# The token quad beside the last softmax: the order of its third and fourth product

## The chip, the cores and the metric

The kernel runs on one core of a Trainium2 chip. The time is the device time of one execution in microseconds, lower is better. Before the change it is 1221.77 us, the median of three runs (1220.72 to 1221.81).

## The reference, cut to what matters

One layer of a hybrid encoder over a sequence of 2048 positions with 1024 channels, in float32:

```python
h = rmsnorm(x, norm_g[l])
proj = h @ w_in[l]
qk_raw, v, o, z_a, gates, u, z_b, qc, z_c = jnp.split(proj, _OFFS, axis=-1)
y_a = mlstm_branch(qk_raw, v, o, ig, fg, ...) * jax.nn.silu(z_a)
y_b = pool_branch(u, pool_w[l], pool_scale[l]) * jax.nn.silu(z_b)
y_c = mem_attn_branch(qc, mem, mem_norm_g[l], w_mem_kv[l]) * jax.nn.silu(z_c)
x = x + jnp.concatenate([y_a, y_b, y_c], axis=-1) @ w_out[l]
```

and a last RMSNorm. The memory attention is a softmax over 256 memory tokens for each of four heads. The change lies in the product `proj`, in the 512 columns of z_a, which the kernel computes while the last head's softmax runs.

## The kernel before, in words

The sequence is worked in two halves of 1024 positions (s = 0 and 1), each in two blocks of 512. The input projection is computed by a Strassen-like scheme: a product of a 2x2 block matrix (two blocks of positions, two halves of the channels) by a 2x2 block of weights is done with seven block products instead of eight. Such a group of seven is a *quad* (class `Quad`, line 224). The x operands of the seven are A11, A12, S1, S2, S3, S4, A22 and the weight operands B11, B21, T1, T2, T3, B22, N4; S and T are sums and differences of blocks. Each operand is split into a high and a low part, and each product is three matmuls for each 128 channels (`mm3`, lines 152, 155 and 156 of the page).

There are four kinds of quads. Channel quads (`qk`, `pool`, `att`) give transposed results; token quads (`tok`, i = 0 for v, 1 for o, 2 for z_a) give results by position. `run_tok` (line 390) runs a token quad: for each product n, for two PSUM banks, 24 matmuls of 128x256 a bank, 48 a product, then an eviction by ScalarE or VectorE. Seven products share four accumulators: P (A11, then A12), U (S2), V (S1, then S4), W (S3, then A22). P and V take PSUM banks of the group "mm" (four banks), U and W of "pt" (two); the other two banks are "aux" (`bank`, line 95).

The order of the products is a table, `TOK_ORDER` (line 49): A11, A12, S2, S1, S3, S4, A22. The results add up across products: the eviction of S2 makes u2 = S2 + A11 product, that of S1 makes S1 + u2, S3 adds to that, S4 and A22 add to u2. The order of the weight operands follows from the same table: `stream` (line 323) lists every form of every quad in order, `prep` (line 280) makes or loads them four forms or so ahead, as the buffers "wf" and "wr" come free when a product is done (`used`). In the first half the forms are made from raw weights (differences on GpSimd and VectorE, splits on ScalarE line 307 and VectorE line 308) and written to DRAM; in the second half they are loaded back.

In each half, `attention_stage` runs four attention quads and then the token quad i = 2 (line 921), the *tail quad*. The last attention quad hands the second block's query to `attend` (line 746), whose steps are emitted by a counter of ticks, one tick behind each bank of the tail quad: scores (two halves), transposes of the softmax output (line 776, two halves of four, into two "pt" banks), the copies of these into a high part th (ScalarE, line 781) and a low part tl (VectorE, line 782), and the product with the values (lines 152 to 156 with th and tl). With `pinned=True` the first matmul of each part of a bank keeps its place in program order.

The tile framework plans the order of instructions on every engine with a simulated timeline; program order is the priority, an instruction goes when its operands and its buffer are free in the plan. Each engine then runs its list in order.

In the second half the tail quad also has steps (`last_step`, line 999): with each product it scales and splits output weights (`prep_wo`, line 966, its work at lines 977 to 982) into the slots of x operands that are used up: the first two into those of A12, then S2, S1, S3, S4, A22. The last stage follows, an output product of 2048x1536 by 1024 columns beside the chunked mLSTM; `load_chunk` (line 1043) brings its inputs, among them qk.

Of the kernel before, what the change touches and what calls it, by code (L numbers as in the profile page):

```python
# [15 lines left out]
ALU = mybir.AluOpType  # L16
# [30 lines left out]
CH_ORDER = (("A11", "B11", "P", True), ("S2", "T2", "U", True), ("A12", "B21", "P", False),  # L47
            ("S1", "T1", "V", True), ("S3", "T3", "W", True), ("S4", "B22", "V", False), ("A22", "N4", "W", False))
TOK_ORDER = (("A11", "B11", "P", True), ("A12", "B21", "P", False), ("S2", "T2", "U", True),
             ("S1", "T1", "V", True), ("S3", "T3", "W", True), ("S4", "B22", "V", False), ("A22", "N4", "W", False))  # L50


def hybrid_block(tc, xT, xn, memT, wch, wuT, wtok, wgt, wkm, wvm, wo, pw, cols, bg, gf, out):
    nc = tc.nc
    V, A, G, T = nc.vector, nc.scalar, nc.gpsimd, nc.tensor
# [4 lines left out]
    def r32(t):  # L60
        return t.bitcast(F32)
# [7 lines left out]
    def tick():  # L69
        now[0] += 1  # L70
        ready = [f for t, f in due if t <= now[0]]
        due[:] = [(t, f) for t, f in due if t > now[0]]
        for f in ready:
            f()
# [12 lines left out]
    with ExitStack() as outer:  # L87
# [7 lines left out]
        def bank(shape, tag):  # L95
            return ps.tile(list(shape), F32, name=tag, tag=tag, bufs={"mm": 4}.get(tag, 2))
# [44 lines left out]
        def ev(name, dtype=F32, shape=(P, BW), tag=None):  # L141
            tag = tag or (name if name in ("s1", "u2") else "e")
            return ep.tile(list(shape), dtype, name=name, tag=tag, bufs=1 if tag == "e" else 2)
# [7 lines left out]
        def mm3(po, ah, al, bh, bl, first, last, pin=False):  # L151
            ins = T.matmul(po, ah, bh, start=first, stop=False, skip_group_check=True)  # L152
            if pin:
                tc.keep_in_program_order(ins)
            T.matmul(po, ah, bl, start=False, stop=False, skip_group_check=True)  # L155
            T.matmul(po, al, bh, start=False, stop=last, skip_group_check=True)  # L156
# [67 lines left out]
        class Quad:  # L224
            def __init__(self, kind, s, i):
                self.kind, self.s, self.i = kind, s, i
                self.tok = kind == "tok"
                self.order = TOK_ORDER if self.tok else CH_ORDER
                self.cost = 2 if self.tok else 1
                self.forms = {}  # L230
                self.held = {}
                self.raw = {}
                self.kept = not (self.tok and i == 0)
# [46 lines left out]
            def prep(self, f):  # L280
                if self.s and self.kept:
                    out = []
                    for kept in cache[self.kind, self.i, f]:
                        t = self.slot(f)
                        dma(r32(t).rearrange("p a b c -> p (a b c)"), kept)
                        out.append(t)
                    self.views(f, out)
                    return
                B = self.raw
                if f == "T2":  # L290
                    G.tensor_tensor(B["B11"], B["B12"], B["B11"], ALU.subtract)  # L291
                    B["T1"] = B["B11"]
                    t2 = wb.tile([P, 4, 256 if self.tok else P], F32, name="wt2", tag="wt2", bufs=1)
                    V.tensor_tensor(t2, B["B22"], B["T1"], ALU.subtract)
                    B["T2"] = t2
                if f == "T3":
                    V.tensor_tensor(B["B12"], B["B22"], B["B12"], ALU.subtract)
                    B["T3"] = B["B12"]
                if f == "N4":
                    G.tensor_tensor(B["B21"], B["B21"], B["T2"], ALU.subtract)  # L300
                    B["N4"] = B["B21"]
                src = B[f]
                out, kept = [], []
                for kk in range(self.cost):
                    t = self.slot(f)
                    part = src[:, 2 * kk:2 * kk + 2] if self.tok else src
                    A.activation(t[:, 0], part, AF.Copy)  # L307
                    V.tensor_tensor(t[:, 1], part, r32(t[:, 0]), ALU.subtract)  # L308
                    out.append(t)
                    if self.kept:  # L310
                        n = f"d_{self.kind}{self.i}{f}{kk}"
                        d = dp.tile([P, D], F32, name=n, tag=n)
                        dma(d, r32(t).rearrange("p a b c -> p (a b c)"))
                        kept.append(d)
                cache[self.kind, self.i, f] = kept
                self.views(f, out)
# [33 lines left out]
        def used(q, f):  # L350
            for tag in q.held.pop(f):
                room[tag] += 1
            pump()
# [36 lines left out]
        def run_tok(q, step=None, pinned=False):  # L390
            n_, s = q.i, q.s
            func = (AF.Copy, AF.Sigmoid, AF.Silu)[n_]
            banks = {}
            s1, u2 = [None, None], [None, None]

            def store(t, i, j, bk):
                dma_out(d_tok[2 * s + i][2 * bk:2 * bk + 2, :, n_ * GW + 256 * j:n_ * GW + 256 * j + 256].rearrange("t p w -> p t w"),
                        t.rearrange("p (t w) -> p t w", t=2))

            for n, (xfm, wfm, acc, opens) in enumerate(q.order):  # L400
                if step is not None:
                    step(n)
                if opens:
                    tag = "mm" if acc in ("P", "V") else "pt"
                    banks[acc] = [bank([P, 2, 256], tag) for _ in range(2)]
                for bk in range(2):
                    pp = banks[acc][bk]
                    for r in range(2):
                        sl = slice((2 * bk + r) * P, (2 * bk + r + 1) * P)
                        for k in range(4):  # L410
                            wh, wl = q.forms[wfm][k]
                            xt = xf[xfm][k]
                            mm3(pp[:, r], xt[:, 0, sl], xt[:, 1, sl], wh, wl, opens and k == 0 and r == 0, k == 3,
                                pin=k == 0 and (opens and r == 1 or pinned and r == 0))
                    pf = pp.rearrange("p a b -> p (a b)")
                    if n == 0:
                        s1[bk] = ev("s1")
                        A.activation(s1[bk], pf, AF.Copy)
                    elif n == 1:
                        c11 = ev("c11", tag="u2")  # L420
                        A.activation(c11, pf, func)
                        store(c11, 0, 0, bk)
                    elif n == 2:
                        u2[bk] = ev("u2")
                        V.tensor_tensor(u2[bk], pf, s1[bk], ALU.add)
                    elif n == 3:
                        V.tensor_tensor(s1[bk], pf, u2[bk], ALU.add)
                    elif n == 4:
                        t = s1[bk]
                        V.tensor_tensor(t, pf, t, ALU.add)  # L430
                        if n_:
                            A.activation(t, t, func)
                        store(t, 1, 1, bk)
                    elif n == 5:
                        t = ev("c12", tag="s1")
                        V.tensor_tensor(t, pf, u2[bk], ALU.add)
                        if n_:
                            A.activation(t, t, func)
                        store(t, 0, 1, bk)
                    else:  # L440
                        t = u2[bk]
                        V.tensor_tensor(t, pf, t, ALU.add)
                        if n_:
                            A.activation(t, t, func)
                        store(t, 1, 0, bk)
                    if bk == 1:
                        used(q, wfm)
                    tick()
# [172 lines left out]
        for n in range(12):  # L621
            later(n + 1, lambda n=n: first(n))
        it = iter(quads)
        run_tok(next(it), pinned=True)
        flush()
        close(mcm)
# [314 lines left out]
        def turn(n):  # L941
# [4 lines left out]
            else:  # L946
# [4 lines left out]
                xf.clear()  # L951
                xf.update(old)
        run_tok(next(it), turn)
        xs["A22"]()
        new["A22"] = xf["A22"]
# [309 lines left out]
```

## Time and profile before

| | |
|---|---|
| median of three runs | 1221.77 us |
| profiled execution | 1220.8 us |
| its span, first to last instruction | 1218.9 us |
| TensorE busy | 1173.5 us, 96% |
| weight loads busy (beside the matmuls) | 1016.1 us, 83% |
| VectorE busy | 743.9 us, 61% |
| ScalarE busy | 480.5 us, 39% |
| GpSimd busy | 211.5 us, 17% |
| mean granted TensorE clock | 0.983 of 2.4 GHz |

Times inside the profile are microseconds from the span's start. A matmul's duration is modelled and overlaps the next; the distance of two starts is what one costs. The tail quad's S2 starts at 406.92 in the first half and at 844.30 in the second. Behind an instruction stand in brackets the idle time of its engine ahead of it and what ended that.

### The profile page before, as it was taken

The page shows a single profiled execution, that of the slowest core. Times are in us where ns is not written, and L with a number is a line of the kernel's source. Part 1 is how long each engine was busy: PE and PEld are TensorE (multiplying, and loading weights), DVE is VectorE, ACT ScalarE, POOL GpSimd, SP SyncE. Part 2 cuts the span into 40 slices and gives each one's busy share as a digit, 9 for nine tenths or more (in the row PEclk, how much of TensorE's full clock was granted, in tenths as well). Part 3 has the DMA queues.
Part 4 walks back from the last instruction along what each step waited for, and adds up shares of the span by engine and source line. Part 5 has one row for each costly group of instructions (what it writes and reads, how often), then busy time and mean ns, then how long its engine had stood idle before and what let it go on. Part 6 is the DMA issues. An engine that isn't in the chain of part 4 may idle for free. (4 is left out here: it accounts for less than half of the span.)

```text
span 1218.9 us, 17628 instructions
## 1 busy us (share of the span) xinstructions
PE 1173.5 (96%) x6579; PEld 1016.1 (83%) x6579; DVE 743.9 (61%) x1324; ACT 480.5 (39%) x947; POOL 211.5 (17%) x154
## 2 busy tenths in 40 slices
PE   6769999999999999999999999999999999999997
PEld 5759888887888998998788888888978888888886
DVE  5966587887777559633564554554546656556444
ACT  7534544444766444331311225555433223222211
POOL 1351121112001003100000000000054423233110
PEclk9879999999999999999999999999999999999999
DMA  9618788779555796546667776446695454554411
GB/s 350 233 44 299 265 293 281 259 276 324 211 195 182 256 390 226 181 140 228 198 219 241 240 244 226 154 155 223 214 325 188 137 184 154 172 165 151 144 52 69
DMA packets 124725, 258.75 MB, mean 212 GB/s; under 512 B 9824, under 2 KB 66400, under 8 KB 124384
## 3 DMA queue, kind: packets, MB, share of 16 engines
q1 hardware_dynamic: 83232, 226.17, 53.9%
q10 hardware_dynamic: 41408, 31.46, 8.1%
q8 instruction: 52, 0.85, 0.3%
q14 instruction: 33, 0.27, 0.1%
HBM read 158.96 MB, written 98.63 MB: 211 GB/s over the span
## 5 line engine op out<-in xcount | busy, mean ns | idle before, releaser
L307 ACT ACTIVATE wf<-wr 128x512 fp32r<-128x512 f32 x120 | 74.3, 627 | 106.7 <-PE mm L156 56.1
L308 DVE TENSOR_TENSOR wf<-wr,wf 128x512 fp32r<-128x512 f32 x120 | 84.8, 716 | 35.2 <-ACT wf L307 35.1
L152 PE MATMUL mm<-xS,wf 128*128 128x512 f32 x256 | 101.3, 396 | 1.9 <-DVE s L377 1.9
L156 PE MATMUL mm<-xS,wf 128*128 128x512 f32 x256 | 101.7, 397 | 0.0
L155 PE MATMUL mm<-xS,wf 128*128 128x512 f32 x256 | 101.0, 395 | 0.0
L1025 PE MATMUL mm<-woh,ybh 128*128 128x512 f32 x256 | 94.8, 405 | 0.0
L1025 PE MATMUL mm<-wol,ybh 128*128 128x512 f32 x256 | 92.8, 397 | 0.0
L1025 PE MATMUL mm<-woh,ybl 128*128 128x512 f32 x256 | 89.9, 394 | 0.0
L152 PE MATMUL mm<-xA,wf 128*128 128x512 f32 x224 | 88.6, 396 | 0.0
L156 PE MATMUL mm<-xA,wf 128*128 128x512 f32 x224 | 87.9, 393 | 0.0
L155 PE MATMUL mm<-xA,wf 128*128 128x512 f32 x224 | 87.7, 392 | 0.0
L1129 DVE SCALAR_TENSOR_TENSOR hh<-hh,ss,gz 128x128 f32<-128x128 f32 x64 | 52.4, 878 | 31.1 <-POOL ss L1127 31.1
L647 DVE SCALAR_TENSOR_TENSOR cacc<-text,col,cacc 128x1024 f32<-128x1024 f32 x48 | 65.5, 1374 | 6.7 <-ACT cacc L644 6.5
L996 POOL TENSOR_TENSOR ybl<-yr,ybh 128x1024 fp32r<-128x1024 f32 x16 | 39.2, 2450 | 173.2 <-ACT ybh L995 169.7
L291 POOL TENSOR_TENSOR wr<-wr 128x512 f32<-128x512 f32 (+1 forms) x16 | 27.2, 1697 | 198.8 <-DVE wf L308 180.4
L152 PE MATMUL pt<-wf,xS 128*128 128x256 f32 x192 | 55.7, 290 | 5.7 <-ACT xS L198 4.6
L156 PE MATMUL pt<-wf,xS 128*128 128x256 f32 x192 | 55.5, 289 | 5.2 <-DVE xS L199 5.2
L156 PE MATMUL mm<-wf,xA 128*128 128x256 f32 x192 | 56.3, 293 | 3.7 <-DVE xA L199 3.7
L152 PE MATMUL mm<-wf,xA 128*128 128x256 f32 x192 | 57.1, 297 | 2.0 <-DMA wf<-d_tok1B 2.0
L152 PEld LDWEIGHTS mm<-xS,wf 128*128 128x128 f32 x256 | 48.5, 189 | 12.0 <-DVE s L377 2.4
L156 PEld LDWEIGHTS mm<-xS,wf 128*128 128x128 f32 x256 | 48.6, 190 | 10.9
L155 PEld LDWEIGHTS mm<-xS,wf 128*128 128x128 f32 x256 | 48.5, 189 | 10.1
(314 smaller groups left out, 3251.3 us busy)
## 6 DMA issues: line engine op xcount, KB each, us to landing
wr<-in_wch_dram SPq DMA_DIRECT2D x20, 512.0 KB, 5.8
y<-in_xT_dram SPq DMA_DIRECT2D x32, 256.0 KB, 6.9
wr<-in_wtok_dram SPq DMA_DIRECT2D x16, 512.0 KB, 6.0
d_qk<-cacc ACTq DMA_DIRECT2D x32, 256.0 KB, 4.5
yr<-d_y SPq DMA_DIRECT2D x16, 512.0 KB, 4.7
qk<-d_qk SPq DMA_DIRECT2D x16, 512.0 KB, 4.1
gz<-d_t SPq DMA_DIRECT2D x16, 512.0 KB, 3.7
xr<-in_xn_dram SPq DMA_DIRECT2D x16, 512.0 KB, 3.6
```

Source lines behind the costliest of these rows:

```text
L152: ins = T.matmul(po, ah, bh, start=first, stop=False, skip_group_check=True)
L155: T.matmul(po, ah, bl, start=False, stop=False, skip_group_check=True)
L156: T.matmul(po, al, bh, start=False, stop=last, skip_group_check=True)
L291: G.tensor_tensor(B["B11"], B["B12"], B["B11"], ALU.subtract)
L307: A.activation(t[:, 0], part, AF.Copy)
L308: V.tensor_tensor(t[:, 1], part, r32(t[:, 0]), ALU.subtract)
L647: V.scalar_tensor_tensor(c, t[:, i:i + 2 * BW], w(i), c, ALU.mult, ALU.add)
L996: G.tensor_tensor(yl, yr, r32(yh), ALU.subtract)
L1025: T.matmul(outs[c][n], l, w[:, n * 512:(n + 1) * 512], start=i == 0 and p_ == 0, stop=i == KO - 1 and p_ == 2)
L1129: V.scalar_tensor_tensor(hh[:, h], hh[:, h], ss[:, h:h + 1], gz[:, 1, h], ALU.mult, ALU.mult)
```

## The change

A second table, `TAIL_ORDER`, is `TOK_ORDER` with its third and fourth entry exchanged: A11, A12, S1, S2, S3, S4, A22. Token quads with i = 2 use it, which is the tail quad of each half. `prep` makes the difference T1 with whichever of T1 and T2 comes first. In `run_tok` the evictions are chosen by the operand's name instead of its place; the sum of S1 with u2 is done at n = 3, in the old order behind S1's bank, in the new one behind S2's bank and its own eviction, reading V's bank that S1 left.

```diff
+TAIL_ORDER = TOK_ORDER[:2] + (TOK_ORDER[3], TOK_ORDER[2]) + TOK_ORDER[4:]
...
-                self.order = TOK_ORDER if self.tok else CH_ORDER
+                self.order = CH_ORDER if not self.tok else TAIL_ORDER if i == 2 else TOK_ORDER
...
-                if f == "T2":
+                if f in ("T1", "T2") and "T1" not in B:
                     G.tensor_tensor(B["B11"], B["B12"], B["B11"], ALU.subtract)
                     B["T1"] = B["B11"]
+                if f == "T2":
                     t2 = wb.tile([P, 4, 256 if self.tok else P], F32, name="wt2", tag="wt2", bufs=1)
                     V.tensor_tensor(t2, B["B22"], B["T1"], ALU.subtract)
...
-                    elif n == 2:
-                        u2[bk] = ev("u2")
-                        V.tensor_tensor(u2[bk], pf, s1[bk], ALU.add)
-                    elif n == 3:
-                        V.tensor_tensor(s1[bk], pf, u2[bk], ALU.add)
-                    elif n == 4:
+                    elif xfm in ("S2", "S1"):
+                        if xfm == "S2":
+                            u2[bk] = ev("u2")
+                            V.tensor_tensor(u2[bk], pf, s1[bk], ALU.add)
+                        if n == 3:
+                            V.tensor_tensor(s1[bk], banks["V"][bk].rearrange("p a b -> p (a b)"), u2[bk], ALU.add)
+                    elif xfm == "S3":
```

## Rows read from the trace of the kernel before

**Rows 1.** The page, busy us of each engine (share of the span), instructions.

```profile
PE 1173.5 (96%) x6579; PEld 1016.1 (83%) x6579; DVE 743.9 (61%) x1324; ACT 480.5 (39%) x947; POOL 211.5 (17%) x154
```

**Rows 2.** TensorE in time, second half: start, duration, line, output<-inputs, count [idle <-releaser].

```profile
828.88 0.60 PE L776 MATMUL pt<-ident,pe 128*128 128x128 f32 x4
829.24 0.36 PE L152 MATMUL aux<-kmhl,qh 128*128 128x256 f32 x1
...
840.55 1.03 PE L776 MATMUL pt<-ident,pe 128*128 128x128 f32 x8
843.57 0.49 PE L152 MATMUL aux<-th,vmhl 128*128 128x512 f32 x1 [1.99 <-ACT th L781]
844.30 0.58 PE L152 MATMUL pt<-wf,xS 128*128 128x256 f32 x1 [0.23 <-DVE tl L782]
...
851.29 0.28 PE L152 MATMUL mm<-wf,xS 128*128 128x256 f32 x1
...
857.98 0.28 PE L152 MATMUL pt<-wf,xS 128*128 128x256 f32 x1
...
863.63 0.28 PE L152 MATMUL mm<-wf,xS 128*128 128x256 f32 x1
```

**Rows 3.** TensorE in time, first half.

```profile
404.23 1.03 PE L776 MATMUL pt<-ident,pe 128*128 128x128 f32 x8
406.15 0.49 PE L152 MATMUL aux<-th,vmhl 128*128 128x512 f32 x1 [0.89 <-ACT th L781]
406.92 0.39 PE L152 MATMUL pt<-wf,xS 128*128 128x256 f32 x1 [0.27 <-DVE tl L782]
...
412.48 0.28 PE L152 MATMUL mm<-wf,xS 128*128 128x256 f32 x1
```

**Rows 4.** Stretches: bounds, length, busy us of PE PEld DVE ACT POOL, PEclk, DMA, GB/s.

```profile
404.00:412.50 8.50, 7.34 (x62) 6.79 (x61) 3.28 (x5) 2.96 (x6) 0.00 (x0) 1.00 0.89 315
840.00:851.00 11.00, 8.78 (x61) 8.23 (x61) 5.57 (x8) 4.65 (x7) 0.07 (x1) 0.84 0.89 310
```

**Rows 5.** ScalarE and VectorE in time, second half, around the hole.

```profile
841.87 0.58 ACT L421 ACTIVATE c<-mm 128x512 f32<-128x512 f32 x1
...
842.92 1.09 ACT L781 ACTIVATE th<-pt 128x512 fp32r<-128x512 f32 x2 [0.48 <-ACT c L421]
844.26 1.15 ACT L981 ACTIVATE woh<-woraw,col 128x1024 fp32r<-128x1024 f32 x1 [0.26 <-DMA woraw<-in_wo_dram]
...
843.55 1.29 DVE L782 TENSOR_TENSOR tl<-pt,th 128x512 fp32r<-128x512 f32 x2 [0.33 <-ACT th L781]
...
848.77 0.69 DVE L425 TENSOR_TENSOR u<-pt,s 128x512 f32<-128x512 f32 x1 [2.04 <-PE pt L156]
```

**Rows 6.** VectorE in time, first half: the last split of T2.

```profile
383.65 0.68 DVE L308 TENSOR_TENSOR wf<-wt,wf 128x512 fp32r<-128x512 f32 x1
```

**Rows 7.** TensorE in time, first half, behind the quads.

```profile
464.48 0.39 PE L152 MATMUL mm<-wf,xA 128*128 128x256 f32 x1 [2.01 <-DMA wf<-d_tok1B]
```

**Rows 8.** ScalarE, VectorE, DMA queue and TensorE in time, from tail quad to last stage.

```profile
850.53 1.06 ACT L977 ACTIVATE woh<-woraw 128x1024 fp32r<-128x1024 f32 x1 [5.12 <-DMA woraw<-in_wo_dram]
...
866.66 1.15 ACT L981 ACTIVATE woh<-woraw,col 128x1024 fp32r<-128x1024 f32 x1 [2.02 <-PE mm L156]
867.72 0.61 ACT L432 ACTIVATE s<-s 128x512 f32<-128x512 f32 x1
...
872.63 0.69 DVE L436 TENSOR_TENSOR c<-mm,u 128x512 f32<-128x512 f32 x1 [2.90 <-DMA d_t<-s]
...
881.94 1.29 DVE L982 SCALAR_TENSOR_TENSOR wol<-woraw,col,woh 128x1024 fp32r<-128x1024 f32 x1 [1.07 <-ACT woh L981]
...
874.55 1.52 SPq L975 DMA_DIRECT2D woraw<-in_wo_dram  x2
...
883.25 0.33 SPq L1047 DMA_DIRECT2D qk<-d_qk  x1
...
887.61 0.60 PE L1083 MATMUL aux<-qk 128*128 128x128 f32 x3 [0.72 <-DMA qk<-d_qk]
```

More of the change, by code (lines that the diff above doesn't have):

```diff
@@ L415, in run_tok @@
                     pf = pp.rearrange("p a b -> p (a b)")
-                    if n == 0:
+                    if xfm == "A11":
                         s1[bk] = ev("s1")
                         A.activation(s1[bk], pf, AF.Copy)
-                    elif n == 1:
+                    elif xfm == "A12":
                         c11 = ev("c11", tag="u2")
@@ L433, in run_tok @@
                         store(t, 1, 1, bk)
-                    elif n == 5:
+                    elif xfm == "S4":
                         t = ev("c12", tag="s1")
```

## The prediction, made before the change was run

> **What bounds the kernel now.** I read four views in this order: the busy shares of the engines, the list of what TensorE waited for, TensorE's instructions in order of time around the two places that the change touches, and then ScalarE, VectorE and the DMA queue at the same places. TensorE is busy 1173.5 us of a span of 1218.9 [rows 1], so some 45 us of it is idle, and only a hole in TensorE's stream, or a stretch at its lower clock, can be won back. The changed quad runs twice, once in each half of the sequence. In both runs the rows show one hole, always at the same instruction: right behind the eight transposes of the last head's softmax (line 776). The third product, S2, wants the two "pt" banks, and the transposes have just filled them; S2 starts only when ScalarE (th, line 781) and VectorE (tl, line 782) have copied the first of them out. In the second run TensorE idles 1.99 and 0.23 us there [rows 2], in the first 0.89 and 0.27 us [rows 3]. After the longer hole the granted clock is 0.84 over the stretch, so part of it ran at 1.2 instead of 2.4 GHz; after the shorter one it stays at 1.00 [rows 4].
>
> **The change, part by part.**
>
> *The swap.* The tail quad now runs S1 before S2. S1 accumulates into bank group V, which takes "mm" banks; the product S2 that needs "pt" banks comes one product later. No matmul is added or removed: 7 products of 48 on either side. What goes is the hole. I size it by start times, which hold idle time and slow clock together. Second run: from the first transpose at 840.55 to the first matmul of S1 at 851.29 is 10.74 us. The work in it is eight transposes, 2 x 0.36 = 0.72 us by the distance from 828.88 to 829.24 for four; one product of the attention output, at most its 0.49 us; and the 48 matmuls of S2, 5.65 us by the undisturbed product from 857.98 to 863.63. That leaves 10.74 - 0.72 - 0.49 - 5.65 = 3.88 us lost [rows 2], of which 6.99 - 5.65 = 1.34 us is the slower clock of S2 itself. First run: 404.23 to 412.48 is 8.25 us, and 8.25 - 0.72 - 0.49 - 5.65 = 1.39 us lost, with S2 itself at full speed (412.48 - 406.92 = 5.56) [rows 3]. The two holes are worth 5.27 us. That is the upper end of the gain.
>
> *What is late next at that place.* The second four transposes are due behind S1's first bank, so the copies th and tl then run under S1's second bank, half a product, 2.83 us. Before, the first tl was done at about 843.55 + 0.64 = 844.19, that is 2.9 us after the transposes' end at 841.27 in the second run, with ScalarE kept until 842.45 by another eviction (c, line 421) [rows 5]; in the first run the same distance is the 406.92 at which S2 could start less 404.95, 2.0 us [rows 3]. So the first run is covered, and the second lacks from 0.1 us up to 1.2 us if ScalarE's 1.15 us scaling of an output weight (woh, line 981) comes ahead of th. I take 0.3 us, nearer to the first, as that scaling started on a weight that landed only at 844.26.
>
> *The two evictions.* V's sum (line 427) needs u2, so it is done behind S2's eviction (line 425) of the same bank: two VectorE operations of 0.69 us [rows 5] fall due together instead of a product apart. The count stays. S3 opens the pt bank of U again and waits only for the first of them; S2's second bank (2.83 us) lies in between, so this costs 0. Without that cover it is 2 x 0.69 = 1.4 us for a run of the quad. V's bank is next written by S4, two products later, and the "mm" group has four banks for P and V; nothing opens a fifth before the quad ends, so no wait is added. The Trainium skill, "PSUM — Partial Sum Buffer", section "Summary: rules for kernel authors", says the opposite of what is done here: evacuate promptly. By it the sum would lose up to that 1.4 us in each run, 2.8 in all; by the rows it loses nothing.
>
> *Weights.* In the first half the difference T1 is still made on GpSimd ahead of both forms, and is now split before T2 instead of behind it. T2's last split ended at 383.65 + 0.68 = 384.33, 20 us ahead of the hole [rows 6], so T1's now is as early and T2's has about a product more than it needs: cost 0, and if the cover were gone, one form's split. In the second half both forms are loaded back; each comes from SP in the new order, same bytes.
>
> *Handed back later.* First run: behind this quad the next weights are the limit once, TensorE waits 2.01 us at 464.48 for a form read back from DRAM [rows 7]. If that landing does not move, the whole 1.39 us is swallowed there; if it follows TensorE (its load waits for a buffer that a product frees), nothing is. I take 0.7, the middle, as both are near. Second run: TensorE reaches the last stage and waits 0.72 us for the first qk at 887.61, whose load went out at 883.25, right after the last output weight was scaled at 881.94 + 1.29 [rows 8]. Between 0 and the full 3.58 us can be swallowed; I take 0.5, because the chain that ends there follows TensorE at several steps (the scaling at 866.66 waited 2.02 us for a product; the eviction at 872.63 for the store of a result).
>
> *The sum.* 5.27 - 0.3 - 0.7 - 0.5 = 3.8 us. The profiled execution took 1220.8 us around its span of 1218.9; 1220.8 - 3.8 = 1217.0. The median of the runs shown is 1.0 us above the profiled one, so 1218.0 by it. The two ends: 1220.8 - 5.27 + 1.0 = 1216.5 with nothing handed back, 1221.8 with all. Instruction order on each engine is planned for the whole program at once, so moving two products may shuffle others; from the rows I can only bound that by a wait like those above, 1 to 2 us either way.
>
> **Rivals.**
>
> *A. The last stage does not start earlier.* If the load at 883.25 stays where it is, all of the second run's gain becomes a longer wait for qk at 887.61. For it: TensorE already waited there, and the scaling of output weights runs in pairs with a DMA between (850.53, then 866.66) [rows 8], not by TensorE's pace alone. Against it: the waits on TensorE in the same rows. Time: only 0.7 us of the first run is left, 1221.1 by the median. Chance 0.20.
>
> *B. Slower: the x tiles of S2 are held one product longer.* The third and fourth output weights are scaled into the slots of S2's input. Before, S2 ended at 851.29 and ScalarE began that scaling at 850.53. Now S2 ends at 840.55 + 0.72 + 2 x 5.65 = 852.6 at the earliest, about 854 with the attention product before it, so the pair starts some 2 us later. Each later pair waits for the raw tiles of the one ahead, so the last pair's load, 874.55 in the old rows, goes 2 us later too and qk at 885.3. TensorE would then stand for several us, and the lower clock behind such a hole costs the 1.34 us seen above: +2.0 + 1.3 - 0.7 = +2.6, 1224.4 by the median. It decides from the point at which that load is issued later than 874.55. Behind the waiting scaling on ScalarE stand the quad's own evictions. The same page of the Trainium skill, section "Engine vs sequencer instructions", calls ScalarE's queue strictly first in, first out; by that rule those evictions cannot pass it. The trace agrees: an eviction of S3 starts at 867.72, only behind the scaling that waited [rows 8]. Against B: between the old pairs there is slack (2.02 us at 866.66 was a wait for TensorE, not for the raw weight), and a new plan can set the evictions ahead. Chance 0.13.
>
> *C. The hole only moves.* The plan could put all eight transposes together again, or the softmax half could be late, and S2 stands behind S1 for about 1 us in each run. For it: the eight were issued together before. Against it: S1's banks are free, so nothing stops its first bank from going between. The gain is then some 1.2 us of 5.27: 1220.6 by the median. Chance 0.13.
>
> **How the numbers follow.** The forecast, 1218.0, has 0.54, with a range of its own from 1215.5 to 1219.8. What a measurement of this kernel can tell from no change is about 0.2%, 2.4 us: faster is below 1219.3, slower above 1224.2. Most of the forecast's chance is faster (0.50), and 0.04 of A and C; the rest of these is no change, 0.30; slower is most of B and 0.04 for a reshuffled order, 0.16. The range from 1215.0 to 1222.5 takes in the upper end of the gain with 1.5 us for the order, A and C, and leaves out B.
>
> **What would show it.** Right: behind A12 of the tail quad four transposes, 24 matmuls into an mm bank, four transposes, 24 more, and S2 with no idle of over 0.5 us; granted clock 1.00 there in the second run; VectorE lines for U and V back to back; S1 and S2 done by 854.5 where they were at 857.98. For A: a wait for qk of over 3 us. For B: the load of the last pair of output weights later than 874.55. For C: an idle of 1 us or more ahead of the first matmul of S2. It is wrong altogether if the quad's stretch got shorter by 3 us or more and the time did not, with no longer wait behind it.

## The result, and the profile after

The changed kernel takes 1239.53 us (median of 4 executions, 1238.72 to 1241.59) against 1221.24 us (4 executions, 1219.48 to 1221.81) for the kernel before on the same chip: ratio 1.0155, 95% interval 1.0137 to 1.0172. It is slower by some 18 us, where a gain of 3.8 us was forecast. The profiled execution took 1239.5 us around a span of 1237.6. The page says little by itself; TensorE's busy time rises from 1173.5 us [rows 1] by 8 us although it runs the same 6579 matmuls, so part of the loss is slower matmuls and the rest idle:

```profile
PE 1181.4 (95%) x6579; PEld 1023.5 (83%) x6579; DVE 740.5 (60%) x1324; ACT 481.9 (39%) x949; POOL 211.9 (17%) x154
```

At the two places that the change touches it does exactly what was forecast. TensorE in time after the change, first half and then second half (start, duration, line, output<-inputs, count; an idle time would stand in brackets):

```profile
404.37 0.60 PE L779 MATMUL pt<-ident,pe 128*128 128x128 f32 x4
...
407.55 0.60 PE L779 MATMUL pt<-ident,pe 128*128 128x128 f32 x4
407.90 0.37 PE L153 MATMUL mm<-wf,xS 128*128 128x256 f32 x1
...
410.72 0.40 PE L153 MATMUL aux<-th,vmhl 128*128 128x512 f32 x1
410.96 0.28 PE L153 MATMUL pt<-wf,xS 128*128 128x256 f32 x1
...
848.11 0.60 PE L779 MATMUL pt<-ident,pe 128*128 128x128 f32 x4
848.46 0.36 PE L153 MATMUL mm<-wf,xS 128*128 128x256 f32 x1
...
851.38 0.60 PE L779 MATMUL pt<-ident,pe 128*128 128x128 f32 x4
...
854.55 0.40 PE L153 MATMUL aux<-th,vmhl 128*128 128x512 f32 x1
...
856.18 0.28 PE L153 MATMUL pt<-wf,xS 128*128 128x256 f32 x1
```

Four transposes, half of S1, four transposes, the other half, then S2 without an idle time: the holes of [rows 2, 3] are gone. The same stretches of the new trace as in [rows 4], and two more, are these (bounds, length, busy us of PE PEld DVE ACT POOL, granted clock, DMA share, GB/s):

```profile
404.00:412.50 8.50, 8.50 (x76) 8.45 (x75) 4.00 (x6) 3.96 (x7) 0.00 (x0) 1.00 0.88 320
847.00:858.00 11.00, 11.00 (x90) 10.69 (x89) 5.10 (x7) 4.37 (x7) 0.38 (x1) 1.00 0.88 305
490.00:500.00 10.00, 6.97 (x40) 6.30 (x40) 5.65 (x13) 4.97 (x9) 0.20 (x1) 0.83 0.68 229
880.00:940.00 60.00, 50.51 (x238) 41.91 (x238) 27.68 (x58) 19.00 (x47) 19.43 (x13) 0.86 0.75 249
```

The first two are full and at 2.4 GHz. The other two, far from the change, show where the time went: TensorE is idle, and part of the rest ran at 1.2 GHz. To follow the loss I matched the TensorE matmuls of both traces and took the start after less the start before, as a median per 20 us: the shift. It is +0.1 at 400, -1.4 at 440 (first hole won: 1.6), +0.2 at 480 (all of it back), +7.5 at 580, +7.6 at 820, +5.6 at 860 and +18.7 from 940 to the end. Behind the second hole nine matmuls of the output projection were also brought forward (9 x 0.23 = 2.1 us), so that hole was worth 2.0 + 2.1 = 4.1 us. So 5.7 us were won and 24 lost: 1.7 between 440 and 480, 7.3 between 480 and 580, 15 between 860 and 940. The waits of TensorE at these places:

```profile
465.32 0.58 PE L153 MATMUL mm<-wf,xA 128*128 128x256 f32 x1 [4.65 <-DMA wf<-d_tok1B]
...
496.52 0.58 PE L153 MATMUL mm<-wf,xA 128*128 128x256 f32 x1 [2.69 <-ACT s L420]
...
892.27 0.79 PE L1028 MATMUL mm<-woh,ybh 128*128 128x512 f32 x1 [2.74 <-ACT ybh L998]
...
896.33 2.08 PE L1086 MATMUL aux<-qk 128*128 128x128 f32 x8 [1.99 <-DMA qk<-d_qk]
...
919.61 0.45 PE L1137 MATMUL aux<-ident,hh 128*128 128x128 f32 x1 [3.41 <-DVE hh L1132]
```

Those at 496 and in the last stage have their cause in the order of other engines' instructions and loads; the one at 465 is taken up with the run e11_s_behind.

*At 496.* ScalarE after the change (ACTq is ScalarE issuing a DMA):

```profile
489.50 0.37 ACTq L399 DMA_DIRECT2D d_t<-c  x1
...
490.64 0.63 ACT L441 ACTIVATE c<-c 128x512 f32<-128x512 f32 x1
...
495.87 0.60 ACT L420 ACTIVATE s<-mm 128x512 f32<-128x512 f32 x1 [3.55 <-DMA d_t<-c]
495.94 0.37 ACTq L399 DMA_DIRECT2D d_t<-c  x1
```

and before, at the same place:

```profile
494.29 0.37 ACTq L397 DMA_DIRECT2D d_t<-c  x1
...
495.31 0.60 ACT L418 ACTIVATE s<-mm 128x512 f32<-128x512 f32 x1 [0.44 <-ACT u L444]
496.51 0.60 ACT L418 ACTIVATE s<-mm 128x512 f32<-128x512 f32 x1 [0.60 <-DMA d_t<-c]
```

After the change the next quad's first eviction s stands ahead of the store of a result that had been ready since 491.27; s itself waits 3.55 us for the buffer that the store ahead of it (489.50) is still reading. Before, both stores were out first.

*In the last stage.* The program comes to the second half's quad 7.6 us late, and this shift has to be taken off before a time is compared. ScalarE's third output weight was scaled at 850.53 [rows 8] and is now scaled at

```profile
862.03 1.06 ACT L980 ACTIVATE woh<-woraw 128x1024 fp32r<-128x1024 f32 x1 [8.26 <-PE pt L157]
```

because it goes into the x tiles of S2, which TensorE now reads until just before. Less the shift that is 854.4, or 3.9 us later. SP's queue follows it:

```profile
864.94 18.00 SPq L978 DMA_DIRECT2D woraw<-in_wo_dram  x6
884.40 0.80 SPq L992 DMA_DIRECT2D yr<-d_y  x2
...
889.22 0.32 SPq L1050 DMA_DIRECT2D qk<-d_qk  x1
```

Six raw-weight loads, each waiting for the tile of an earlier one, hold the queue until 882.94. Behind them stand two loads yr, the rows of the pooling and memory branches (ScalarE and GpSimd split them into ybh and ybl for the output product), and the qk load. ScalarE's first copy ybh waits for the second yr, which went out at 884.82:

```profile
891.16 2.00 ACT L998 ACTIVATE ybh<-yr 128x1024 fp32r<-128x1024 f32 x2 [3.29 <-DMA yr<-d_y]
```

Before, it went out at

```profile
876.17 0.37 SPq L989 DMA_DIRECT2D yr<-d_y  x1
```

Less the shift, yr now goes out at 877.2 (876.17 before) and qk at 881.6 (883.25 before), so neither is late by much. But TensorE, without the hole, comes 4 us earlier by the same count: its shift is +3.5 until the wait at 892.27. The queue did not follow it, and what the hole gave goes into the waits for ybh and qk, 2.74 + 1.99 us where one of 0.72 stood before [rows 8]. GpSimd has another order too, after:

```profile
892.30 4.67 POOL L999 TENSOR_TENSOR ybl<-yr,ybh 128x1024 fp32r<-128x1024 f32 x2 [17.73 <-DMA gfb<-in_gf_dram]
897.10 1.26 POOL L1068 TENSOR_TENSOR Ab<-Ab,mask 128x512 f32<-128x512 f32 x1
...
914.46 2.36 POOL L999 TENSOR_TENSOR ybl<-yr,ybh 128x1024 fp32r<-128x1024 f32 x1 [9.07 <-ACT ybh L998]
916.92 1.02 POOL L1130 TENSOR_TENSOR ss<-ss,mhalf 128x4 f32<-128x4 f32 x1
```

and before:

```profile
889.05 1.30 POOL L1065 TENSOR_TENSOR Ab<-Ab,mask 128x512 f32<-128x512 f32 x1 [3.22 <-DMA Ab<-d_a]
890.31 2.40 POOL L996 TENSOR_TENSOR ybl<-yr,ybh 128x1024 fp32r<-128x1024 f32 x1
...
899.58 1.03 POOL L1127 TENSOR_TENSOR ss<-ss,mhalf 128x4 f32<-128x4 f32 x1 [2.72 <-DVE ss L1126]
903.68 2.36 POOL L996 TENSOR_TENSOR ybl<-yr,ybh 128x1024 fp32r<-128x1024 f32 x1 [3.08 <-PE pt L1098]
```

Before, the mask of chunk 0 went ahead of the second 2.4 us subtraction ybl, and the power ss of chunk 0's norm ahead of the third. After, ybl goes first both times; hh waits for ss, and TensorE's transposes wait for hh (3.41 us at 919.61).

### The profile page after: what moved, and what is told of

Its sections match the earlier page's. It is cut to its first block, busy times and chain, and to the rows that moved or that the text cites. A ratio compares the mean times of both kernels' runs of the same rounds, so it can differ in the third digit from the quotient of the medians.

```text
span 1237.6 us, 17631 instructions
## 1 busy us (share of the span) xinstructions
PE 1181.4 (95%) x6579; PEld 1023.5 (83%) x6579; DVE 740.5 (60%) x1324; ACT 481.9 (39%) x949; POOL 211.9 (17%) x154
## 5 line engine op out<-in xcount | busy, mean ns | idle before, releaser
L1028 PEld LDWEIGHTS mm<-woh,ybh 128*128 128x128 f32 x256 | 48.6, 191 | 12.2 <-ACT ybh L998 3.2
L153 PEld LDWEIGHTS mm<-xS,wf 128*128 128x128 f32 x256 | 48.5, 189 | 12.2 <-DVE s L379 2.4
L1028 PEld LDWEIGHTS mm<-woh,ybl 128*128 128x128 f32 x256 | 48.5, 190 | 10.8
```

The source lines that it names most:

```text
L1028: T.matmul(outs[c][n], l, w[:, n * 512:(n + 1) * 512], start=i == 0 and p_ == 0, stop=i == KO - 1 and p_ == 2)
```

## Experiments

On the later chips single executions spread over 8 to 12 us, also of the kernel before, and a shift of -1.6 to +4.5 us arises before 400 us, where the program is the same. So each run is read twice: by its ratio, and by how its shift grows within a stretch of the trace. "Lost from 820" is the shift at 960 less that at 820; the new kernel has +11.2 there.

**Which half.** The swap in one half alone:

```
-  self.order = CH_ORDER if not self.tok else TAIL_ORDER if i == 2 else TOK_ORDER
+  ... TAIL_ORDER if i == 2 and s == 0 else TOK_ORDER      # e1_first
+  ... TAIL_ORDER if i == 2 and s == 1 else TOK_ORDER      # e2_second
```

> The new order in the first half's tail quad alone; the second half's keeps the old order. Theory W (what was lost behind the second tail quad, some 13 us, comes from the output weights that wait for S2's input slots): the last stage is as before, so the loss is that of the first half alone: 1.4 won in the hole, given back at the wait for the weights read back (464 us), about 4 lost at the eviction that waits on ScalarE for a store (490 to 500 us), 3.3 by the slower pace of TensorE behind it: about +7.5, 1229 us. Rival P (the whole plan is shifted by the first change, and the last stage suffers whatever the second quad does): +18, 1239 us.

Measured 1226.62 us, ratio 1.0045 (1.0026 to 1.0064). The hole gives 1.6, 440 to 580 loses 6.2, and from 820 nothing is lost (-0.7).

> The new order in the second half's tail quad alone. Theory W: everything up to 830 us as before, 4 us won in the hole at 840, 13 lost between 880 and 930: about +9, 1230 us, with the last pair of output weights loaded some 3 us later behind the quad's end than before. Rival P: the second quad alone is a gain of 3 to 4 us, 1217.5 us.

Measured 1231.35 us, ratio 1.0092 (1.0063 to 1.0121). Nothing lost before 820, +10.8 from 820. The losses of the halves lie apart: the first half's own plan makes those at 465 and 496, the second half's those of the last stage. By the ratios they add up to 1.4 of the 1.55%; in the traces e1_first loses less from 440 to 580 than the new kernel (6.2 against 8.9 us), and some 2 us of this is a slower pace of TensorE, told in the last section.

**The output weights' tiles.** The third and fourth output weights take the tiles of S1, now free first, and S2's go to the next two:

```
-  wslots = [8, 10, 4, 6, 12, 14, 16, 18, 20, 22, 24, 26]
+  wslots = [8, 10, 12, 14, 4, 6, 16, 18, 20, 22, 24, 26]
```

> The change in both halves, and the third to sixth output weight exchanged in their places: the pair that is scaled first goes into the slots of S1's input, which is now used up first, the next pair into those of S2. Theory W: most of the 13 us behind the second quad come back, the 7.5 us of the first half stay, the 4 us won at 840 stay: 1222 to 1228 us. Rival P: no difference from the change, 1238 to 1240 us. A second rival, that the two evictions behind one bank hold the quad's results and so the last stage: also 1238 to 1240 us.

Measured 1232.66 us, ratio 1.0099 (1.0072 to 1.0126): 7.0 lost from 820 instead of 11.2. The wait for ybh is gone: yr goes out at 881.06 and qk at 888.13, which is 2.5 us earlier than before by this trace's shift of 7.4. Slower than expected, so the tiles are not all of it.

> The new order in the second half alone, with the output weights' slots exchanged as in the run before. Theory W: the hole of 4 us at 840 is won and the last stage starts that much earlier: 1217 to 1219 us, faster than both kernels. Rival P: 1217.5 us too, so that it and the second half alone would be the same. If the evictions were the cause: 1230 us.

Measured 1225.35 us, ratio 1.0035 (1.0012 to 1.0059). A miss. The shift at 880 is -3.0, so quad and weights are right there, and then it grows to +4.7. GpSimd's and TensorE's rows of this run say why:

```profile
900.64 2.34 POOL L999 TENSOR_TENSOR ybl<-yr,ybh 128x1024 fp32r<-128x1024 f32 x1 [6.66 <-PE pt L1101]
903.08 1.03 POOL L1130 TENSOR_TENSOR ss<-ss,mhalf 128x4 f32<-128x4 f32 x1
```

```profile
905.76 0.42 PE L1137 MATMUL aux<-ident,hh 128*128 128x128 f32 x1 [4.04 <-DVE hh L1132]
```

ybl stands ahead of ss although the weights are in time: a second cause. The mirror of the tiles' test is the old kernel with the new tiles (the wslots edit alone, S1 being its later product):

> The kernel before, with its old order of products, but the third and fourth output weights put into the x tiles that S1 frees instead of S2's: in this kernel S1 is the LATER of the two, so it has the weights of the changed kernel without its swapped products. Theory W (weights that wait for the later product's x tiles delay the raw-weight loads, the qk load and the whole last stage): the wait before the scale of the third weight grows from 5.1 to about 8 us, the qk load is issued some 5 us later, and the time is 1226 to 1232. Rival (the plan as a whole shifts with the swap, the weights have slack): 1219 to 1222.

Measured 1227.48 us, ratio 1.0047 (1.0024 to 1.0071), 8.9 lost from 820 without any swap. The third weight comes at

```profile
859.58 1.06 ACT L977 ACTIVATE woh<-woraw 128x1024 fp32r<-128x1024 f32 x1 [11.66 <-PE mm L156]
```

and TensorE then waits for ybh and qk:

```profile
889.79 0.50 PE L1025 MATMUL mm<-woh,ybh 128*128 128x512 f32 x1 [1.35 <-ACT ybh L995]
893.79 1.36 PE L1083 MATMUL aux<-qk 128*128 128x128 f32 x8 [2.81 <-DMA qk<-d_qk]
```

Time, place and the weight's delay (6.6 us by its own shift of 2.4) are those of theory W; the qk load, at 887.07, is only 1.4 us later by the same count and not 5, so that part of the expectation failed. What waits first is ybh, whose yr went out at 882.71, 4.1 us later by that count. GpSimd's first two ybl also stand together in this plan, so the 8.9 us are not the tiles' alone.

**GpSimd's order.** The second half swapped with the new tiles, and the subtraction of chunk 3 moved off GpSimd:

```
-  G.tensor_tensor(yl, yr, r32(yh), ALU.subtract)
+  (V if c == 3 else G).tensor_tensor(yl, yr, r32(yh), ALU.subtract)      # e6_low_dve
```

> The second half swapped alone, S1's x tiles for the third and fourth weights (1225.4 in the run before, the quad's 3 us won and 7.7 us lost in the last stage), and the low part of the memory rows of chunk 3 subtracted on VectorE instead of GpSimd. Theory G (GpSimd's order: that 2.3 us subtraction stands ahead of the power of chunk 0's norm, hh is scaled late and TensorE's transposes wait): the 4.0 us wait for hh at 906 falls below 1 us and the time is 1218.5 to 1221.5. Rival (hh is late because the gate masks or the eviction before it are late): the wait stays at 4 and the time at 1224 to 1226.

Measured 1221.74 us, ratio 1.0013 (0.9989 to 1.0036), 0.2 us above what theory G expected; the shift changes by -0.8 from 820 where e4_second_slots lost 4.4. ss comes at 899.35, and TensorE's waits for hh shrink from 5.6 to 3.3 us in sum, the first of them from 4.04 to 1.34 and not below 1 us. Then also chunk 2's subtraction held behind the masks:

```
+  if c == 2:
+      tc.keep_in_program_order(lo)          # lo: chunk 2's subtraction;  e7_gp_order
```

> The same with GpSimd's other change undone as well: the low part of chunk 2 is held behind the masks of chunks 0 and 1, as it is (behind that of chunk 0) in the kernel before. Theory G says that both together cost the 7.7 us: 1216.5 to 1219, faster than the kernel before by 2 to 4 us. Rival (only the power counts): the same time as the run with chunk 3 alone, within 0.7.

Measured 1221.37 us, ratio 0.9993 (0.9974 to 1.0013); -3.9 from 820 in the trace, no wait for hh left:

```profile
895.27 2.39 POOL L999 TENSOR_TENSOR ybl<-yr,ybh 128x1024 fp32r<-128x1024 f32 x1
898.03 1.03 POOL L1132 TENSOR_TENSOR ss<-ss,mhalf 128x4 f32<-128x4 f32 x1 [0.37 <-DVE ss L1131]
```

So in the traces the last stage's loss is taken apart: 10.8 with the second half alone, less 6.5 by the tiles, less 5.2 by chunk 3, less 3.1 by chunk 2 (2.1 and 2.9 in the two later traces of this kernel). The trace came out as theory G had it. The median did not: 1216.5 to 1219 was expected, and 0.4 us below e6_low_dve is what the rival had.

**Is the closed hole then worth anything?** The same kernel twice more, and its control, the old kernel with only the two GpSimd edits:

> The kernel before, its products and its output-weight tiles untouched, with only the GpSimd edits of the run e7_gp_order (chunk 3's low part on VectorE, chunk 2's held behind the masks). It tells whether those edits win by themselves. If they only put back an order that the kernel before already has: 1220.5 to 1222.5, no difference. Rival (the last stage before was itself held by GpSimd): 1218 to 1219.5, and then e7_gp_order's gain is not the swap's.

> The kernel of e7_gp_order again, whose profiled execution was 3.7 us ahead of the kernel before at the end while its median was only 0.5 us below, on a chip where single executions spread over 8 us. If the profiled execution tells the kernel: 1216.5 to 1219, ratio 0.996 to 0.998. If the median does: 1220 to 1222.

> The kernel of e7_gp_order a third time, beside the others on one chip: two timings gave 0.9993 and 1.0000 of the kernel before, while two traces put its end 2.9 and 3.9 us ahead from 820 on. If the traces tell it: 0.996 to 0.998. If the timings do: 0.999 to 1.001.

> The kernel before with the GpSimd edits alone, again, as the partner of e15_gp_order_third: the difference of the two is the swap of the second half with its weight tiles, GpSimd's order held the same. If the 2.2 us hole is worth what the traces show, e15 is 1.5 to 3 us below this one; if the timings of e9 and e10 tell it, the two are equal within 1.2 us.

The old kernel with the GpSimd edits: 1218.81 us, 0.9985 (0.9964 to 1.0006), and 1218.69 us, 0.9973 (0.9959 to 0.9986), in the range of the rival of e9_before_gp. With swap and tiles on top: 1219.96 us, 1.0000 (0.9981 to 1.0019), and 1219.75 us, 0.9987 (0.9968 to 1.0007). The traces change by -1.7 and -2.7 from 820 without the swap, by -3.9, -2.9 and -3.7 with it: 1.3 us better on average. The medians stand 1.1 us the other way, inside their spread. So the repaired swap is not shown to win anything, and the only version here that is shown to beat the kernel before, by 0.1 to 0.4% in one of its two timings, has no swap in it.

**The first half at 496.** First the tile: the first result of the quad ahead in a tile of its own, on top of e1_first.

```
-  t = ev("c12", tag="s1")
+  t = misc([P, BW], "c12") if bk == 0 and step and not pinned else ev("c12", tag="s1")
```

> The first half swapped alone (1226.6 in the run before: hole won, 5.1 lost between 460 and 570), and the first of the two S4 results of the next token quad in a tile of its own, so that the following quad's first eviction s does not wait for that result's store. Theory T (that eviction, waiting for the store's landing ahead of the issue of the second store on ScalarE, holds TensorE at 495 and the rest follows from this hole): the waits of TensorE for s (3.5 us in sum) fall below 1 us and the time is 1219.5 to 1222.5. Rival (the weight loads, which run about 2 us later there, are what holds it): the hole is filled by another wait near 496 and the time stays at 1225 to 1227.

Measured 1232.11 us, ratio 1.0085 (1.0051 to 1.0118). It failed as a test: the plan moved s further forward still, to 491.19, where it waited for an older store, and TensorE's waits for s summed to 4.9 us. Then the order itself: s ordered behind the issue of the store of u.

```
+  if bk == 0 and len(held) == 1:             # held: the first store of u of the quad ahead
+      tc.add_manual_dep(lo.ins, held.pop().ins.name, NoSync)     # lo: s, line 420
```

> The first half swapped alone (1226.6), with the first eviction s of the following token quad ordered behind the issue of the first store of the quad ahead, as ScalarE has it in the kernel before; nothing else. Theory T (the order of ScalarE at 490 to 500 holds TensorE for 3.5 us and what follows grows from there): the waits for s fall below 1 us and the time is 1220 to 1223. Rival L (the stores land late because the weight loads of that stretch run late; the order is not the point): waits of 2 us or more remain there and the time is 1225 to 1228.

Measured 1223.46 us, ratio 1.0020 (1.0006 to 1.0035). 480 to 580 now costs nothing (-0.03, after 5.4 in e1_first), s runs at 493.24, and no wait of TensorE for it is left. For the waits theory T holds; the time is half a us above its range. What stays is one wait:

```profile
465.14 0.58 PE L153 MATMUL mm<-wf,xA 128*128 128x256 f32 x1 [5.39 <-DMA wf<-d_tok1B]
```

The weights read back here were stored only at 454.86, not 451.43: VectorE makes them (line 310) at 454.15, behind 5.4 us of row scalings (line 192), where the old plan made them at 450.71, ahead of the scalings. So the scalings behind the weights:

```
+  tc.add_manual_dep(sc.ins, lows[-1].ins.name, NoSync)   # sc: first scaling, lows: weight splits
-  if n == 0:   # the scalings are called here,
+  if n == 2:   # two products later, so that the splits are known
```

> The first half swapped alone, with ScalarE's order at 490 put back (the run e11_s_behind, 1223.5; in its trace the hole is won, shift -2.5, and a wait of 5.4 us at 465 for the reloaded weights d_tok1B takes it and 2.3 us more), and now the 5.4 us of row scalings of the next x blocks held on VectorE behind the weight splits that feed that store and reload (they stood ahead of the splits since the swap; in the kernel before they stood behind). Theory V (VectorE's order makes the weights 3.4 us late): the store is issued at about 451 instead of 455, the wait at 465 falls to 2 us or less, and the time is 1218.5 to 1221. Rival (the transfers themselves are late, or the later scalings hold the x splits): a wait of 4 us or more stays between 455 and 500 and the time is 1222 to 1226.

Measured 1225.03 us, ratio 1.0028 (1.0010 to 1.0045): a miss. The wait for the weights is gone, and two others stand in its place:

```profile
465.69 0.36 PE L153 MATMUL mm<-wf,xA 128*128 128x256 f32 x1 [2.14 <-ACT xA L202]
469.79 2.08 PE L169 MATMUL aux<-dg,ones 128*128 128x512 f32 x2 [3.13 <-DVE dg L167]
```

VectorE's order was why the weights came late, but it owes both pieces of work in that stretch; I found no order that gets the 1.6 us out of it.

**All together.** Both halves swapped with the repairs of e7_gp_order and e11_s_behind, and with the scalings as well:

> Both halves swapped, with the repairs of e7_gp_order in the last stage and of e11_s_behind at 490. If the repairs are additive: about 0 to 2 us for the first half on top of e10_gp_order_again, so 1217 to 1221. If the first half's loss is not the order of ScalarE: 1221 to 1225.

Measured 1221.13 us, ratio 1.0016 (0.9997 to 1.0035). -1.2 from 820 instead of +11.2, -0.3 at 480 to 580 instead of +7.3. So with the named orders put back the 18 us are gone. But a part of that is what the GpSimd edits give by themselves: on the same chip the old kernel with them (e9_before_gp) took 1218.81 us, 2.3 less than this one. Of what is still lost, 3.6 us lie at 440 to 480.

> Both halves swapped with all four repairs (output-weight tiles, GpSimd's order, ScalarE's order at 490, VectorE's order at 450). If theory V holds: 1216 to 1219, faster than the kernel before by 2 to 4 us. If not: 1220 to 1224.

Measured 1223.84 us, ratio 1.0020 (1.0002 to 1.0039): not the gain of theory V, as e13_scale_later has it.

## Why the prediction was wrong

- *The holes: right.* 5.27 us were forecast, 1.6 + 4.1 = 5.7 came. The quad went in the forecast order, th and tl made nobody wait (0.3 was taken for them), the two evictions cost nothing, and the second stretch kept its full clock. One size in it was luck: 1.34 of the 3.88 us was slow clock, and the run e8_c12 has the same hole without it (last section).
- *Handed back at 464: mis-sized.* 0.7 was taken between 0 and 1.39. All of it went, and the cause was on neither side of that bound: the weights came later than before, by VectorE's order (e11_s_behind: 3.9 us from 440 to 480, more than the hole gave).
- *Handed back in the last stage: mis-sized.* 0.5 was taken between 0 and 3.58, because the chain there was read as following TensorE. TensorE came 4 us earlier, the loads of yr and qk did not follow, and the waits for them rose from 0.72 to 4.73 us: all that the hole gave was handed back.
- *The step that failed* is the last one of the sum: that moving two products may shuffle others, bounded "by a wait like those above, 1 to 2 us either way". The shuffle is the result. It cost 7.3 us at 480 to 580 (ScalarE's eviction ahead of a store, shown by e11_s_behind; some 2 us of the 7.3 may be the pace of the last section) and, of the last stage, what GpSimd's order cost: 8.2 us, as the loss from 820 falls from 7.0 in e3_slots to -1.2 in e12_both (behind 860 the same edits gave the old kernel only 0.0 and 0.9 us). I bounded the length of a wait, and not how many queues could each get one, nor what stands behind each.
- *Rival B began right and went on wrong.* It named the tiles and had the third weight at about 854, where it is less the shift (854.4), and the tiles cost 4.2 us (11.2 less 7.0) with both halves swapped, 6.5 with one. But the delay did not go down its chain: less the shift, the last raw-weight load went out at 875.0 (875.74 before) and qk at 881.6, not at 885.3. The sign from which it decides, a load of the last pair later than 874.55, came by the clock alone (880.27 and 882.61), by the 7.6 us lost in the first half. Its +2.6 us priced a late qk; what the tiles cost is a queue that did not follow TensorE, with the slower clock of 880 to 940 (0.86) on top.
- *A* came true in part: the last stage's loads did not start as much earlier as TensorE. Its sign, a wait for qk of over 3 us, did not come (1.99), as 2.74 us of wait stood at ybh ahead of it. *C* did not occur: no hole opened ahead of S2.
- *My test for being wrong altogether* (a shorter quad, no gain, and no longer wait behind it) did not apply: the longer waits are there.

What stays open: whether the closed hole is worth its 1.3 us of the traces once the rest is put back; and why the old kernel gains from the GpSimd edits alone (2.1 and 3.0 us by the medians), since in the traces 1.6 to 1.8 us of it lie at 840 to 860, ahead of them, where mainly the clock differs.

## What to carry to other kernels

Where one plan orders every engine's queue, moving one product re-orders all of them; before its gain is counted, go through each in-order queue behind it and ask which short instruction, a store's issue or a small power that another engine waits for, could now stand behind a long or a waiting one. When two products swap, swap whatever inherits their buffers too, and look three stages on for it. A closed hole gives back its length once, and each queue that the new plan orders worse can lose more than that.

## What the runs showed of the hardware

TensorE has two paces of the same matmul at a granted clock of 1.00. These are the same 60 us of dense 128x256 products, before the change,

```profile
500.00:560.00 60.00, 60.00 (x531) 60.00 (x531) 23.41 (x34) 15.41 (x25) 4.80 (x2) 1.00 0.52 174
```

after it,

```profile
500.00:560.00 60.00, 60.00 (x512) 60.00 (x511) 22.02 (x32) 16.01 (x26) 4.80 (x2) 1.00 0.45 150
```

and in two executions of one kernel, e10_gp_order_again

```profile
500.00:560.00 60.00, 60.00 (x512) 60.00 (x511) 22.71 (x33) 16.00 (x26) 4.80 (x2) 1.00 0.49 163
```

and e15_gp_order_third:

```profile
500.00:560.00 60.00, 60.00 (x531) 60.00 (x531) 24.09 (x35) 15.40 (x25) 4.80 (x2) 1.00 0.53 177
```

531 against 512 matmuls, 113.0 against 117.2 ns each, 2.2 us over the stretch. As one kernel shows both, the change does not set the pace, and some 2 of the 7.3 us lost at 480 to 580 in the profiled execution may be this alone. What picks the pace I can't tell: in the trace before it turns at 465, where TensorE stands still, and also near 416, where it does not.

The lower clock behind a hole is not certain either. Before the change, the stretch that holds the waits of 1.99 and 0.23 us was granted

```profile
843.00:853.00 10.00, 9.20 (x65) 8.89 (x66) 4.99 (x7) 4.37 (x5) 0.10 (x1) 0.83 0.80 306
```

and in e8_c12, whose second half is that of the kernel before, the same two waits, to the hundredth,

```profile
851.86 0.50 PE L153 MATMUL aux<-th,vmhl 128*128 128x512 f32 x1 [1.99 <-ACT th L784]
852.59 0.39 PE L153 MATMUL pt<-wf,xS 128*128 128x256 f32 x1 [0.23 <-DVE tl L785]
```

left it at 2.4 GHz:

```profile
851.00:861.00 10.00, 8.91 (x74) 8.60 (x75) 5.58 (x7) 4.25 (x5) 0.00 (x0) 1.00 0.84 319
```

Of the eight traces with this hole, S2 behind it took 7.0 to 7.2 us in three (before, e5_before_slots, e11_s_behind) and 5.6 to 5.8 us in the other five; by the prediction's own sum the hole cost 2.1 to 3.9 us. So its price in one profiled execution, 3.88 us here, holds a part (1.34) that most others don't pay.
